# A state-space block's output: the order of its products, and kernels loaded by 8 transfers

## The chip, the cores and the metric

One core of one Trainium2 chip runs one program. The metric is the device time of one execution in microseconds (us), lower is better. TensorE (PE) multiplies, VectorE (DVE), ScalarE (ACT) and GpSimd (POOL) work element by element, SyncE (SP) issues most of the transfers between the chip's memory and SBUF, and ACT issues a few. A matrix product reads its operands from SBUF and adds into PSUM, eight banks of 128 partitions by 512 float32 each.

## The reference

Two layers; this case touches the state-space mixer of the first one. Cut to what matters:

```python
u = x.reshape(bsz, seq, 64, 16)                  # 64 groups of 16 channels, 512 positions
bu = einsum('blgh,gph->lbgp', u, B)              # complex, 64 states a group
s  = associative_scan(s_l = lambda_bar * s_{l-1} + bu_l)
y  = Re(einsum('lbgp,ghp->blgh', s, C)) + d_skip * x
h  = gelu(y)
val, gate = split(h @ w_glu, 2);  z = val * sigmoid(gate);  mix = z @ w_out
x  = layer_norm(alpha * x + mix)                 # then a SwiGLU and the second layer (attention)
```

All in float32 to a tight tolerance; the kernel splits large matrices into a high and a low part (`wh`, `wl`, `xh`, `xl`) and multiplies three times.

## The kernel before

The scan is done by chunks. The 512 positions are 64 chunks of L = 8. Within a chunk the output is a sum over at most 8 lags, a small convolution kernel; from chunk to chunk only the state is carried. The 64 groups are done in NBLK = 4 blocks of 16 groups (GB = 8 pairs: index j counts pairs, g2 picks one of the two).

For block b the steps are: `f_g`, `f_h` (DVE: tables g and h, two each), `p_t` (PE: transposes of g, ACT copies them), `p_m` (PE: input to state, into banks 2 and 3), `p_k` (PE: the lags, bank 0; ACT copies them to `ksb`; SP writes them to the DRAM scratch `kd` by two transfers, 8 groups each), `f_n` (SP reads `kd` back as the kernel tile `tn`, 128 partitions of 8 lags by 16 channels: row block n is `kd` shifted by 16 n), `f_r`, `f_s` (DVE: the scan; result `s`), `p_y` (PE: the output, banks 6 and 7; ACT copies it to `ysb` in two halves), `p_z` (PE transposes `ysb`, ACT makes the Gelu `hg` and its high part `xh`), `f_l` (DVE: the low part `xl`).

`p_y` makes, for each of 16 groups (j, g2), three products into the same 64 partitions by 128 columns of psum: step 0 is xs (the input, K = 128 rows: 8 lags by 16 channels) with `tn`; steps 1 and 2 are the real and imaginary state with h (K = 64 rows). In the profile these are the shapes 128*64 and 64*64 of L969; each float32 product is two records.

`tn` of blocks 0, 1 and 2 lies in halves of `xl` and `xh` that are not yet in use (`TNX`); that of block 3 in two ring tiles. Each of the 16 groups' kernels is read by 8 row blocks of two halves, so 16 transfers of 64 KB a block. All of them are issued by SP, but block 0's second half by ACT.

The order of the work in this stage is written out by hand as a string of letters (`SSM_ORDER`, one letter a step, the digit the block), and within the stage the scheduler keeps it on all engines:

```
"u1 u1 i1 c2 p p k1 n1 p r1 u1 u1 u1 e2 s1 g2 y1 j2 t2 T2 z1 m2 M2 h2 p i2 c3 k2 n2 u1 e3 r2 l1 p u1 u1 s2 y2 "
"g3 t3 j3 T3 z2 m3 M3 h3 i3 k3 p n3 u1 l2 r3 u1 s3 p q y3 q w0 z3 a w4 l3 q q q"
```

Between the blocks stand parts of the GLU's large products on blocks already done (u, w) and the splits of their weights (p on POOL, q on DVE: `Weights.pump`, L290 and L295). `Weights.load` (L226) issues a load as soon as a ring tile is free. Behind the stage the scheduler orders by itself: `ssm_end` (the rest of the GLU, then the output projection with the LayerNorm). `x_rev` (L1086) is the residual, which overwrites xs, so it waits until the last step 0 of block 3 has read it.

Of the kernel before, what the change touches and what calls it, by code (L numbers as in the profile page):

```python
# [22 lines left out]
L = 8  # L23
NCH = S // L
NBLK = 4
GB = 8
# [283 lines left out]
class Trunk:  # L310
# [341 lines left out]
    def ssm(self):  # L652


        tc, nc, io, ring, ws = self.tc, self.nc, self.io, self.ring, self.ws
# [27 lines left out]
        half = lambda t, i: t[:, i * NG * L:(i + 1) * NG * L].rearrange("p (a g n) -> p a g n", a=2, n=4)  # L683
# [24 lines left out]
        for hf in range(4):  # L708
# [4 lines left out]
        kd = dr.tile([NBLK, 16, 32, 240], F32, name="kd")  # L713
# [4 lines left out]
                          in_=zero.unsqueeze(1).to_broadcast([128, NBLK * 4, 112]))  # L718
# [172 lines left out]
            ring.put(ksb)  # L891

        def f_n(b):
            if b in TNX:
                half = (self.xl, self.xh)[TNX[b]][:, 4:8].rearrange("p k t -> p (k t)").bitcast(F32)
                tn = [half[:, :1024], half[:, 1024:]]
            else:
                tn = [ring.get("tn", F32) for _ in range(2)]
            for hf in range(2):
                for n in range(L):  # L900
                    (nc.scalar if b == 0 and hf else nc.sync).dma_start(
                        out=tn[hf][n * 16:(n + 1) * 16].rearrange("p (g t) -> p g t", g=8),
                        in_=kd[b, hf * 8:hf * 8 + 8, 0:16, n * 16:n * 16 + 128].rearrange("g h t -> h g t"))
            st[b]["tn"] = tn

        def f_e(b):
# [49 lines left out]
        def p_y(b):  # L956
            tn, s, h = st[b]["tn"], st[b]["s"], st[b]["h"]
            yp = self.ps[:, 6:8].rearrange("p a (j t) -> p (a j) t", j=4)
            for j in range(GB):
                for step in range(3):  # L960
                    for g2 in range(2):
                        p0, idx = g2 * 64, j * 2 + g2
                        rows = slice(p0, p0 + 64)
                        if step == 0:
                            a, m_ = xs[:, g2 * NG + b * GB + j], tn[idx // 8][:, (idx % 8) * 128:(idx % 8 + 1) * 128]
                        else:
                            a = s[rows, (step - 1) * 512 + j * 64:(step - 1) * 512 + j * 64 + 64]
                            m_ = h[step - 1][rows, j * 128:(j + 1) * 128]
                        nc.tensor.matmul(out=yp[rows, j], lhsT=a, rhs=m_, start=step == 0, stop=step == 2)  # L969
            ring.put(s, *h)  # L970
            if b not in TNX:
                ring.put(*tn)
            ysb = ring.get("ysb", F32)
            y4 = ysb.rearrange("p (i j h) -> p j i h", i=L, j=GB)
            for hf in range(2):
                js = slice(hf * 4, hf * 4 + 4)
                nc.scalar.activation(y4[:, js], yp[:, js].rearrange("p j (i h) -> p j i h", i=L), AF.Copy)
            st[b]["ysb"] = ysb
# [15 lines left out]
        def f_l(b, e=V):  # L994
            tt(self.xl[:, 2 * b:2 * b + 2], st[b]["hg2"], self.xh[:, 2 * b:2 * b + 2].bitcast(F32), SUB, e)
            ring.put(st[b]["hg"])
# [61 lines left out]
        def pump(e):  # L1058
# [3 lines left out]

        fs = dict(c=a_c, g=f_g, j=lambda b: f_g(b, 1), h=f_h, i=lambda b: f_h(b, 1), d=p_d, t=p_t,
                  T=lambda b: p_t(b, 1), m=p_m, M=lambda b: p_m(b, 1), e=f_e, k=p_k, r=f_r, y=p_y, l=f_l,
                  L=lambda b: f_l(b, G_), n=f_n, s=f_s, z=p_z,
                  B=lambda b: (powers(rest_), G_.memset(scr[0][:, 0:1], 0.0), scr_done()), b=lambda b: (levels(rest_), scr_done()))
        ET = mybir.EngineType
# [376 lines left out]
```

## Time and profile before

| | us |
|---|---|
| three runs | 1207.26, 1207.07, 1202.6 (median 1207.07) |
| the profiled execution | 1201.96 |
| its span | 1200.2 |
| `p_y` of block 0 / 1 / 2 / 3 (first L969 to the next line) | 43.80 to 51.42 / 77.78 to 85.49 / 105.68 to 113.31 / 132.09 to 139.72 |
| granted TensorE clock | 0.998 |

In a timeline line stand start, duration, engine, line, operation, output <- inputs, shape and count; in brackets the idle time of the engine before it and what ended it. In a line of stretches stand the stretch, its length, the busy time of PE, PEld (weight loads), DVE, ACT and POOL with counts, the granted clock, the DMA engines' busy share and GB/s. A line that lists a source line's instructions gives durations as min/median/max in ns and the first and last start in us.

### The profile page before, as it was taken

How to read it: one execution, taken by the hardware profiler on the slowest of the kernel's cores; microseconds unless marked ns; L12 is line 12 of the kernel's file. 1: busy time of each engine (PE TensorE's matmuls, PEld its weight loads, DVE VectorE, ACT ScalarE, POOL GpSimd, SP SyncE). 2: the span in 40 equal slices, each digit the busy share in tenths (PEclk: the TensorE clock that was granted, in tenths of full speed). 3: DMA queues.
4: the chain of work that ended last, by engine and by line, in shares of the span. 5: the costliest groups of instructions: out<-in, count | busy, mean ns of one | idle time of the engine just before them, and what ended most of it. 6: DMA issues, size and time to landing. Idle time of an engine off the chain costs nothing.

```text
span 1200.2 us, 20813 instructions
## 1 busy us (share of the span) xinstructions
PE 1156.9 (96%) x8494; PEld 1035.8 (86%) x8494; DVE 894.0 (74%) x1406; ACT 512.5 (43%) x813; POOL 378.6 (32%) x333
## 2 busy tenths in 40 slices
PE   3899999999999999999999999999999999999996
PEld 3777788899999999888887888878999999998885
DVE  8888585798788777435867787877987778884446
ACT  1355273054444445331156665653444444454300
POOL 6644402036455551001312322221254556510000
PEclk9999999999999999999999999999999999999999
DMA  5433741023323325431201121221233232264201
GB/s 199 115 81 81 233 168 47 1 89 108 122 87 121 109 90 197 137 110 66 106 13 59 54 71 53 72 88 53 89 106 123 72 123 90 88 227 141 70 18 52
DMA packets 44799, 117.91 MB, mean 98 GB/s; under 512 B 6816, under 2 KB 18080, under 8 KB 44576
## 3 DMA queue, kind: packets, MB, share of 16 engines
q1 hardware_dynamic: 43552, 116.07, 28.9%
q8 instruction: 66, 1.08, 0.4%
q10 hardware_dynamic: 1152, 0.52, 0.3%
q14 instruction: 29, 0.24, 0.1%
HBM read 112.51 MB, written 4.06 MB: 97 GB/s over the span
## 4 chain that ended last, share of the span: by engine, by line
PE 83%; DVE 10%; ACT 2%; issue 2%; POOL 2%; DMA 1%; SPq 0%; DVEq 0%; POOLq 0%; ACTq 0%
PE psum L359 16%; PE psum L361 16%; PE psum L360 16%; PE psum L378 8%; PE psum L380 8%; PE psum L379 8%; PE psum L969 2%; DVE nb L1212 1%; PE psum L1234 1%; ACT wh L290 1%; DVE wl L295 1%; PE psum L1299 1%; PE psum L1250 1%; POOL be L1213 1%; PE psum L1249 1%
## 5 line engine op out<-in xcount | busy, mean ns | idle before, releaser
L233 POOL TENSOR_TENSOR wf<-raw,wf 128x1024 fp32r<-128x1024 f32 (+1 forms) x80 | 160.0, 2015 | 128.5 <-ACT wf L246 81.6
L360 PE MATMUL psum<-xf,wf 128*128 128x256 f32 x640 | 181.4, 283 | 0.6 <-DVE wf L233 0.6
L361 PE MATMUL psum<-xf,wf 128*128 128x256 f32 x640 | 181.7, 284 | 0.0
L359 PE MATMUL psum<-xf,wf 128*128 128x256 f32 x640 | 181.5, 284 | 0.0
L295 DVE TENSOR_TENSOR wl<-raw,wh 128x1024 fp32r<-128x1024 f32 x91 | 119.6, 1325 | 59.1 <-ACT wh L290 40.3
L359 PE MATMUL psum<-xh,wh 128*128 128x512 f32 (+1 forms) x416 | 146.0, 352 | 1.8 <-ACT xh L992 1.3
L290 ACT ACTIVATE wh<-raw 128x1024 fp32r<-128x1024 f32 x108 | 112.4, 1054 | 76.1 <-PE psum L380 25.9
L361 PE MATMUL psum<-xl,wh 128*128 128x512 f32 (+1 forms) x416 | 141.4, 343 | 0.5 <-DVE xl L658 0.5
L360 PE MATMUL psum<-xh,wl 128*128 128x512 f32 (+1 forms) x416 | 141.1, 340 | 0.3 <-POOL wl L295 0.3
L380 PE MATMUL psum<-wh,hid 128*128 128x512 f32 x352 | 137.8, 392 | 0.0
L379 PE MATMUL psum<-wl,hid 128*128 128x512 f32 x352 | 137.5, 391 | 0.0
L378 PE MATMUL psum<-wh,hid 128*128 128x512 f32 x352 | 137.4, 390 | 0.0
L359 PE MATMUL psum<-xh,wf 128*128 128x256 f32 x480 | 134.9, 281 | 0.1
L361 PE MATMUL psum<-xl,wf 128*128 128x256 f32 x480 | 134.1, 279 | 0.0
L360 PE MATMUL psum<-xh,wf 128*128 128x256 f32 x480 | 134.1, 279 | 0.0
L360 PEld LDWEIGHTS psum<-xf,wf 128*128 128x128 f32 x640 | 122.3, 191 | 0.8 <-DVE wf L233 0.8
L359 PEld LDWEIGHTS psum<-xf,wf 128*128 128x128 f32 x640 | 122.6, 192 | 0.0
L361 PEld LDWEIGHTS psum<-xf,wf 128*128 128x128 f32 x640 | 122.3, 191 | 0.0
L295 POOL TENSOR_TENSOR wl<-raw,wh 128x1024 fp32r<-128x1024 f32 x17 | 41.9, 2476 | 177.0 <-DVE wl L295 96.6
L462 DVE TENSOR_TENSOR cv<-cv,psum 128x512 f32<-128x512 f32 x80 | 54.6, 683 | 48.6 <-PE psum L361 39.6
L359 PEld LDWEIGHTS psum<-xh,wf 128*128 128x128 f32 x480 | 90.5, 188 | 0.3 <-DVE hid L597 0.3
L361 PEld LDWEIGHTS psum<-xl,wf 128*128 128x128 f32 x480 | 90.3, 188 | 0.0
(227 smaller groups left out, 2679.2 us busy)
## 6 DMA issues: line engine op xcount, KB each, us to landing
raw<-w_gu SPq DMA_DIRECT2D x88, 512.0 KB, 3.4
raw<-w_down SPq DMA_DIRECT2D x44, 512.0 KB, 3.9
raw<-w_glu SPq DMA_DIRECT2D x16, 512.0 KB, 5.0
raw<-w_qk SPq DMA_DIRECT2D x16, 512.0 KB, 3.3
raw<-w_out SPq DMA_DIRECT2D x8, 512.0 KB, 3.4
raw<-w_v SPq DMA_DIRECT2D x8, 512.0 KB, 3.5
raw<-w_o SPq DMA_DIRECT2D x8, 512.0 KB, 3.2
xres<-xs SPq DMA_DIRECT2D x4, 512.0 KB, 6.9
```

Of the source, the lines that this page charges most:

```text
L233: tt = lambda o, a, b, op=SUB, e=V: e.tensor_tensor(out=o, in0=a, in1=b, op=op)
L290: nc.scalar.activation(h, w, AF.Copy)
L295: (self.l_eng or nc.vector).tensor_tensor(out=l, in0=w, in1=h.bitcast(F32), op=SUB)
L359: mm(out=out, lhsT=sh, rhs=mh, start=first, stop=False)
L360: mm(out=out, lhsT=sl, rhs=mh, start=False, stop=False)
L361: mm(out=out, lhsT=sh, rhs=ml, start=False, stop=last)
L378: mm(out=o, lhsT=sh[:, ts], rhs=hl[0][:, c], start=first, stop=False)
L379: mm(out=o, lhsT=sh[:, ts], rhs=hl[1][:, c], start=False, stop=False)
L380: mm(out=o, lhsT=sl[:, ts], rhs=hl[0][:, c], start=False, stop=last)
L462: tt = lambda o, a, b, op=ADD: V.tensor_tensor(out=o, in0=a, in1=b, op=op)
L969: nc.tensor.matmul(out=yp[rows, j], lhsT=a, rhs=m_, start=step == 0, stop=step == 2)
L1212: V.tensor_tensor_scan(nb[:, h], nb[:, h], dm[u], 0.0, MUL, ADD)
```

## The change

In `p_y` the loop over the three steps goes outside the loop over j: first all 16 products with `tn`, then 16 with the real state, then 16 with the imaginary one. The psum start flag is set for the first pair of a bank alone, the stop flag for the last. In `f_n`, blocks 0, 1 and 2 read all 16 groups in one transfer per row block: 8 transfers of 128 KB instead of 16 of 64 KB, in block 0 by turns on SP and ACT. Block 3 keeps its 16.

```diff
         def f_n(b):
+            lags = lambda gs, n: kd[b, gs, 0:16, n * 16:n * 16 + 128].rearrange("g h t -> h g t")
             if b in TNX:
                 half = (self.xl, self.xh)[TNX[b]][:, 4:8].rearrange("p k t -> p (k t)").bitcast(F32)
                 tn = [half[:, :1024], half[:, 1024:]]
+                for n in range(L):
+                    (nc.scalar if b == 0 and n % 2 else nc.sync).dma_start(
+                        out=half[n * 16:(n + 1) * 16].rearrange("p (g t) -> p g t", g=16), in_=lags(slice(0, 16), n))
             else:
                 tn = [ring.get("tn", F32) for _ in range(2)]
-            for hf in range(2):
-                for n in range(L):
-                    (nc.scalar if b == 0 and hf else nc.sync).dma_start(
-                        out=tn[hf][n * 16:(n + 1) * 16].rearrange("p (g t) -> p g t", g=8),
-                        in_=kd[b, hf * 8:hf * 8 + 8, 0:16, n * 16:n * 16 + 128].rearrange("g h t -> h g t"))
+                for hf in range(2):
+                    for n in range(L):
+                        nc.sync.dma_start(out=tn[hf][n * 16:(n + 1) * 16].rearrange("p (g t) -> p g t", g=8),
+                                          in_=lags(slice(hf * 8, hf * 8 + 8), n))
...
         def p_y(b):
-            for j in range(GB):
-                for step in range(3):
+            for step in range(3):
+                for j in range(GB):
                     for g2 in range(2):
...
-                        nc.tensor.matmul(out=yp[rows, j], lhsT=a, rhs=m_, start=step == 0, stop=step == 2)
+                        nc.tensor.matmul(out=yp[rows, j], lhsT=a, rhs=m_, start=step == 0 and j % 4 == 0,
+                                         stop=step == 2 and j % 4 == 3)
```

On PE, `p_y` of block 1 began with these rows, of which the three of L969 came eight times over (xh holds `tn`, h and s are the two operands of the state's products), ahead of the transposes L834 of the next block:

```order
L969 MATMUL psum<-xh,xres 64x128 x2
L969 MATMUL psum<-h_701,s_923 64x128 x2
L969 MATMUL psum<-h_736,s_923 64x128 x2
L834 MATMUL psum<-ident,g_929 128x128 x8
L834 MATMUL psum<-ident,g_984 128x128 x8
L984 MATMUL psum<-ident,ysb_981 128x128 x8
```

```order
L974 MATMUL psum<-xh,xres 64x128 x16
L974 MATMUL psum<-h_693,s_907 64x128 x16
L974 MATMUL psum<-h_728,s_907 64x128 x16
L834 MATMUL psum<-ident,g_913 128x128 x8
L834 MATMUL psum<-ident,g_968 128x128 x8
L990 MATMUL psum<-ident,ysb_965 128x128 x8
```

The shape changes once between the first row and the second, where it changed twice for each j; PE's order is the same everywhere else.

On SP, from block 1's writes of `kd` to block 2's reads (first as before, then as now):

```order
L888 DMA kd<-ksb_754 128x2x128 x2
L901 DMA xh<-kd 16x8x128 x16
L226 DMA raw_859<-w_glu 128x1024
L226 DMA raw_1062<-w_glu 128x1024
L888 DMA kd<-ksb_1070 128x2x128 x2
L901 DMA xl<-kd 16x8x128 x16
```

```order
L888 DMA kd<-ksb_746 128x2x128 x2
L900 DMA xh<-kd 16x16x128 x8
L226 DMA raw_843<-w_glu 128x1024
L226 DMA raw_1046<-w_glu 128x1024
L888 DMA kd<-ksb_1054 128x2x128 x2
L900 DMA xl<-kd 16x16x128 x8
```

The weight loads behind the reads now have 8 issues ahead of them where they had 16. The first read waits for both L888 rows, where it waited for the first.

On ACT, behind block 3's `p_y` (raw_1456 and raw_1686 are weight tiles just loaded, hg and xh the Gelu of block 3 and its high part):

```order
L290 ACTIVATE wh_1618<-raw_1480 128x1024
L989 ACTIVATE hg_1668<-psum 128x8x64 x2
L992 ACTIVATE xh<-hg_1668 128x1024
L290 ACTIVATE wh_1700<-raw_1559 128x1024
L290 ACTIVATE wh_1706<-raw_1565 128x1024
```

```order
L290 ACTIVATE wh_1594<-raw_1456 128x1024
L290 ACTIVATE wh_1797<-raw_1686 128x1024
L995 ACTIVATE hg_1644<-psum 128x8x64 x2
L998 ACTIVATE xh<-hg_1644 128x1024
L290 ACTIVATE wh_1676<-raw_1535 128x1024
```

One split of a weight tile has come ahead of the Gelu, and on DVE its low part ahead of block 3's `xl`. On SP the LayerNorm's scale has gone from ahead of `x_rev` to behind the two weight loads that follow it; raw_1686 is the second of these.

## Prediction

> **What bounds the kernel now.** I read the page first, then the lines of L969 (the products of `p_y`), then the timeline around each of the four places where it runs, then SP's queue.
>
> ```profile
> PE 1156.9 (96%) x8494; PEld 1035.8 (86%) x8494; DVE 894.0 (74%) x1406; ACT 512.5 (43%) x813; POOL 378.6 (32%) x333
> PE 83%; DVE 10%; ACT 2%; issue 2%; POOL 2%; DMA 1%; SPq 0%; DVEq 0%; POOLq 0%; ACTq 0%
> 150.00:200.00 50.00, 50.00 (x220) 41.05 (x219) 38.49 (x47) 30.93 (x38) 5.90 (x4) 1.00 0.38 129
> ```
>
> TensorE is the bound, and it has no idle time in the 50 us behind the state-space stage (the third line is a stretch of the trace: PE busy 50.00 of 50.00). So what PE gains before 140 us moves the end, unless another engine eats it.
>
> ```profile
> L969 PE MATMUL psum<-xl,xres x64: 272/284/324, 43.8 to 112.5; 128*64 128x128 f32 x64
> L969 PE MATMUL psum<-h,s x256: 268/270/321, 44.2 to 139.5; 64*64 64x128 f32 x128
>   issue: 12.8, 64
> 105.68 0.44 PE L969 MATMUL psum<-xl,xres 128*64 128x128 f32 x4
> 106.05 0.66 PE L969 MATMUL psum<-h,s 64*64 64x128 f32 x8
> 106.64 0.44 PE L969 MATMUL psum<-xl,xres 128*64 128x128 f32 x4
> ...
> 113.31 1.09 PE L834 MATMUL psum<-ident,g 128*128 128x128 f32 x8
> 116.55 2.09 PE L845 MATMUL psum<-xres,gt 128*64 128x64 f32 x64
> ```
>
> The first two lines give one record's duration (min/median/max ns), the third L969's idle time: 64 gaps whose releaser is "issue", 16 in each block. The others are `p_y` of block 2. One j takes 0.955 us (106.64 - 105.68 is 0.96; eight take 113.31 - 105.68 = 7.63). Its products with the kernel (L969, 128*64) are 4 records, 52 ns apart ((0.44 - 0.284)/3, 0.284 being one record); those with the state (64*64) are 8 records 55 ns apart ((0.66 - 0.27)/7): 4 x 0.052 + 8 x 0.0557 = 0.65 us. The other 0.30 us are two gaps of 0.15, one at each change between the shapes 128*64 and 64*64. It cannot be accumulation into one address: step 2 follows step 1 into the same psum with no gap, and there is a gap from j to j+1, which write different addresses.
>
> **The change part by part.** *Order.* The products and their count stay. Shape changes per block fall from 16 to 2, so 14 gaps go: 14 x 0.15 = 2.1 us by spacing, 14 x 0.2 (12.8/64) = 2.8 by the idle column. I take 2.2, near the spacing, since starts are measured and ends modelled: `p_y` then takes 5.4 us instead of 7.63. That a run of 32 equal records holds 52 ns is bounded by L845: the same shape 128*64, half the columns, 64 records in 2.09 us, 33 ns each.
>
> The copies to `ysb` lose nothing: the first half waits for step 2 of j = 3, which ends 16 records (0.85 us) before the end, and the copy takes 0.60. But step 0 of all eight j now comes first, so both halves of `tn` are needed within 0.85 us of the start, where the second half had 3.8 us.
>
> *Block 0 gains nothing.*
>
> ```profile
> 43.80 0.44 PE L969 MATMUL psum<-xl,xres 128*64 128x128 f32 x4 [1.15 <-DMA xl<-kd]
> 51.52 1.22 DVE L658 TENSOR_TENSOR g<-g,psum 128x1024 f32<-128x1024 f32 x1
> 51.42 1.09 PE L834 MATMUL psum<-ident,g 128*128 128x128 f32 x8
> 52.89 1.06 PE L834 MATMUL psum<-ident,g 128*128 128x128 f32 x8 [0.37 <-DVE g L658]
> ```
>
> The second group of transposes (T1) waits for DVE's g, done at 51.52 + 1.22 = 52.74, and DVE does not wait for `p_y`. If `p_y` ends near 49 instead of 51.4, PE idles longer before 52.89; all behind it stays. That also covers block 0's transfers up to 2 us of delay.
>
> *Transfers, block 1.* Eight of 128 KB replace sixteen of 64 KB.
>
> ```profile
> xl<-kd SPq DMA_DIRECT2D x24, 64.0 KB, 2.4
> 69.06 1.78 SPq L888 DMA_DIRECT2D kd<-ksb  x2
> L888 SPq DMA_DIRECT2D kd<-ksb x2: 377/846/1315, 69.1 to 69.5; - x2
> DMA to landing us min/median/max: 2.7/2.7/2.8
> 71.76 7.42 SPq L901 DMA_DIRECT2D xh<-kd  x16
> 37.00:37.50 0.50, 0.50 (x7) 0.50 (x6) 0.50 (x2) 0.00 (x0) 0.50 (x2) 1.00 1.01 247
> 77.78 0.44 PE L969 MATMUL psum<-xh,xres 128*64 128x128 f32 x4 [0.18 <-issue]
> 85.49 0.76 PE L834 MATMUL psum<-ident,g 128*128 128x128 f32 x5
> ```
>
> Each transfer now reads all 16 groups, so the first waits for both writes of `kd`: the second is issued at 69.5 and lands 2.7 later, 72.2, against 71.76 now. Sixteen issues take 7.42 us, 0.46 each; eight at that pace end at 72.2 + 3.7 = 75.9. But the same 1 MB must move: 247 GB/s is the most that rows of 512 B reached with all engines full (stretch 37.0 to 37.5, DMA share 1.01), so it needs at least 4.3 us, by 230 GB/s 4.6. With 0.8 until data flow and 1.1 until the landing is seen (2.4 in all for 64 KB, the first line), the last lands at 72.2 + 0.8 + 4.6 + 1.1 = 78.7. PE is there at 77.78: it waits 0.9. Bounds: 0.2 if issue alone sets it, 1.5 for a slower stream. Block 1 gains 2.2 - 0.9 = 1.3.
> [...] The trace's full engines at 247 GB/s decide, so I keep 0.9.
>
> *Block 2.* Its chain ACT `ksb` to `kd` to `tn` hangs on block 1's output, so it moves along. First issue 97.92, with the later second write some 98.3; the last lands at 98.3 + 6.5 = 104.8 on today's clock, and PE comes at 105.68 today; both move by 1.3. No wait: 2.2 more. What is late next is DVE, which moved by 1.3 only:
>
> ```profile
> 116.27 1.22 DVE L658 TENSOR_TENSOR h<-h,psum 128x1024 f32<-128x1024 f32 x1
> 118.78 0.57 PE L879 MATMUL psum<-h,g 64*32 64x112 f32 x16
> 121.67 0.59 PE L879 MATMUL psum<-h,g 64*32 64x112 f32 x16 [0.95 <-issue]
> ```
>
> `p_k` of block 3 needs the second h: ready at 117.49 - 1.3 = 116.2, used (second half of the 118.78 group) at 118.97 - 3.5 = 115.5. It waits 0.8. Later in the same `p_k` PE stands 0.95 us for "issue"; if that runs on during the wait, nothing is lost, else 0.8. I take half: 0.4.
>
> *Block 3 gains nothing.* It keeps 16 transfers, first half first.
>
> ```profile
> 132.09 0.44 PE L969 MATMUL psum<-tn,xres 128*64 128x128 f32 x4 [1.38 <-DMA tn<-kd]
> 135.90 0.44 PE L969 MATMUL psum<-tn,xres 128*64 128x128 f32 x4
> L901 SPq DMA_DIRECT2D tn<-kd x16: 303/428/431, 125.1 to 132.1; - x16
> DMA to landing us min/median/max: 2.5/3.2/3.8
> 139.72 0.50 PE L359 MATMUL psum<-xh,wh 128*128 128x512 f32 x1
> ```
>
> The last issue at 132.1 lands at 135.3 (134.6 to 135.9): hidden now, as j = 4 starts at 135.90. After, on the same clock, step 0 of j = 4 wants it at 132.94 and waits to 135.3; then 0.85 + 0.15 + 3.4 us remain, ending at 139.7, where it ends today. The gaps saved become a wait for `tn`; the bound is 0.6 either way.
>
> *Behind the stage.* ACT's split of a later weight now stands ahead of z3's Gelu.
>
> ```profile
> 139.24 0.33 SPq L1086 DMA_DIRECT2D xres<-x_rev  x1
> 143.81 0.33 SPq L226 DMA_DIRECT2D raw<-w_glu  x1
> DMA to landing us min/median/max: 3.1/4.2/10.1
> 148.08 1.04 PE L984 MATMUL psum<-ident,ysb 128*128 128x128 f32 x8
> 148.87 0.48 PE L359 MATMUL psum<-xh,wh 128*128 128x512 f32 x1
> 154.47 0.39 PE L359 MATMUL psum<-xh,wh 128*128 128x512 f32 x1
> 149.16 2.12 ACT L989 ACTIVATE hg<-psum 128x512 f32<-128x512 f32 x2 [7.78 <-PE psum L984]
> 152.40 1.23 DVE L658 TENSOR_TENSOR xl<-hg,xh 128x1024 fp32r<-128x1024 f32 x1 [8.62 <-ACT xh L992]
> ```
>
> The third line is the landing of the `raw` loads between 120 and 175 us. On today's clock that load is issued at 143.81 and lands at 148.0, the split takes 1.05, and the Gelu could start at 149.1, as it does. xl ends at 153.6. PE has 24 products from 148.87 that don't need block 3; the 25th, at 154.47, needs its xh, the 27th, 0.46 us later, its xl: 1.3 us of delay are covered. Cost 0. x_rev, its wait on `p_y`'s step 0 now ending early, goes ahead of it by more than before, which helps. Other moves on SP, DVE and ACT there are hidden by the 50.00 of 50.00.
>
> Sum: 0 - 1.3 - 2.2 + 0.4 + 0 + 0 = -3.1 us. The profiled execution took 1201.96 us (span 1200.2): 1198.9. The three runs shown are 1207.26, 1207.07 and 1202.6; from their median it would be 1204.0. Both levels occur twice in the four executions, so I put 1202 between them.
>
> **The rivals.** *Issue takes longer for 128 KB (slower).* The second 128 KB write of `kd` took SP 1.315 us, the first 0.377. Its place: `tn` of blocks 1 and 2. At t per issue the last lands at 72.2 + 7t + 2.7 in block 1, a wait of 7t - 2.9, and 7t - 4.6 in block 2. It eats the 4.4 us gained from t = 0.85 on; at 1.3 it costs 6.2 + 4.5 - 4.4 = +6.3, 1208.3. Against it: kd's first write and 64 KB loads at 0.43. Chance 0.16 that waits eat most of the gain (time near 1202), a quarter of it really slower.
>
> *Z3's weight load lands late.* At the 10.1 us seen, 153.9 instead of 148.0, PE would stand 5.9 - 1.3 = 4.6 us: +1.5, 1203.5. Against it: x_rev leaves sooner. Chance 0.08.
>
> *The clock drops in block 0.* PE would idle about 2.4 us before 52.89 around a 1.09 us burst.
>
> ```profile
> 55.00:59.00 4.00, 2.57 (x66) 2.00 (x62) 2.13 (x3) 3.04 (x3) 0.78 (x2) 1.00 0.00 0
> ```
>
> Here PE is busy 2.57 of 4.00 us and the clock granted is 1.00. At half clock the work from 52.89 to 56.84 would take up to 4 us longer: +0.9, 1202.9. Chance 0.04.
> [...]
>
> *More is on the path.* If gaps cost 0.2 (2.8 a block), no `tn` wait grows and block 3 gains as well: 3 x 2.8 = 8.4 less 1 for DVE, 1194.6. Against it: the 247 GB/s and the 135.3. Chance 0.11.
>
> **How the numbers follow.** The forecast (-1 to -5.5 us) has 0.61. What a measurement can tell here is about 0.5%, 6 us: nearly all of the forecast lies inside it. Faster by more: most of the last rival and a little of the forecast, 0.13. Slower by more: a quarter of the first, some of the next two and an unseen cost of the moved weight splits, 0.08. Same: 0.79. Range: 1195 (last rival) to 1209 (the upper level with +2); the forecast's own is 1196.5 to 1206.
>
> **What would show it.** L969's gaps for "issue" fall from 64 to about 8, and `p_y` takes 5.4 us in blocks 0 to 2. PE waits for `xh<-kd` some 0.9 us in block 1 and for the second `tn` some 2.4 us inside block 3's step 0; T1 of block 0 still starts at 52.9. The start of z3's transposes moves from 148.1 to 145.0. The forecast is wrong if products of one shape run slower than 55 ns, if the eight issues take over 6 us, or if PE waits behind 150 us.

## The result and the profile after

The changed kernel took 1215.35 us (median of 4 runs, 1213.41 to 1216.26) against 1205.86 for the kernel before (4 runs, 1202.6 to 1207.26). The ratio is 1.0091 [1.0075, 1.0107]: slower by 0.9%, about 9.5 us, where I had forecast 3 us less and a range that ended at 1209. The profiled execution took 1215.46 us with a span of 1213.6, 13.4 us more than the 1200.2 before.

The page of the changed kernel first: PE's busy time, then the clock granted to PE in 40 slices, where the third and the last had been a 9. Below it are lines of the answer on L974, the products of `p_y` (L969 before): the time of one record, and what ended the idle time in front of it.

```profile
PE 1154.8 (95%) x8494; PEld 1042.2 (86%) x8494; DVE 895.2 (74%) x1406; ACT 512.1 (42%) x813; POOL 379.5 (31%) x333
PEclk9989999999999999999999999999999999999998
L974 PE MATMUL psum<-xh,xres x32: 421/421/474, 84.5 to 87.8; 128*64 128x128 f32 x32
  issue: 21.2, 7
  DMA tn<-kd: 4.0, 2
  DMA xl<-kd: 3.9, 1
```

PE's work is the same (1154.8 against 1156.9 us). The answer on a line counts PE and its weight loads (PEld) together. Of the 64 small gaps for "issue" before, 63 (12.6 of 12.8 us) were idle time of the weight loads; PE itself stood 0.2 us for "issue" and 2.6 for kernels. Now PE stands 5.8 us in one gap for "issue", 7.9 for kernels and 2.0 in block 0 (below); the other 15.4 of the 21.2 us belong to the weight loads. A record of block 1 took 421 ns instead of 283: the work itself ran slower.

The four places in PE's timeline, block 0 to block 3 (start, length, operation, count; in brackets the idle time ahead and what ended it):

```profile
43.68 1.97 PE L974 MATMUL psum<-xl,xres 128*64 128x128 f32 x32 [2.01 <-DMA raw<-w_glu]
52.71 1.94 PE L834 MATMUL psum<-ident,g 128*128 128x128 f32 x8 [2.41 <-DVE g L658]
84.54 3.68 PE L974 MATMUL psum<-xh,xres 128*64 128x128 f32 x32 [5.78 <-issue]
88.15 4.45 PE L974 MATMUL psum<-h,s 64*64 64x128 f32 x64
92.53 1.09 PE L834 MATMUL psum<-ident,g 128*128 128x128 f32 x8
116.63 3.36 PE L974 MATMUL psum<-xl,xres 128*64 128x128 f32 x32 [3.94 <-DMA xl<-kd]
123.78 1.09 PE L834 MATMUL psum<-ident,g 128*128 128x128 f32 x8
143.32 1.09 PE L974 MATMUL psum<-tn,xres 128*64 128x128 f32 x16 [1.78 <-DMA tn<-kd]
146.61 1.09 PE L974 MATMUL psum<-tn,xres 128*64 128x128 f32 x16 [2.19 <-DMA tn<-kd]
147.63 5.38 PE L974 MATMUL psum<-h,s 64*64 64x128 f32 x64
152.94 0.50 PE L359 MATMUL psum<-xh,wh 128*128 128x512 f32 x1
```

PE stands 5.78 us ahead of block 1 and 3.94 ahead of block 2; the 5.78 is marked "issue", but the answer on the tile `xh` lists it as a wait for the transfers into `xh`. Block by block, on the two clocks: `p_y` of block 1 ends at 92.53 instead of 85.49 (+7.0), of block 2 at 123.78 instead of 113.31 (+10.5), and the first product behind block 3 starts at 152.94 instead of 139.72 (+13.2). z3's transposes start at 161.30 instead of 148.08, +13.2 again. So the whole loss arises in the state-space stage; the span is 13.4 us longer, so only 0.2 us is added behind 153 us.

The transfers and the clock in block 1: SP's eight issues (the landing row is that of all 128 KB transfers), then the changed kernel in steps of 2 us, and last a stretch of before. The last three columns are the clock granted to PE, the DMA engines' busy share, and GB/s.

```profile
73.38 3.76 SPq L900 DMA_DIRECT2D xh<-kd  x8
DMA to landing us min/median/max: 3.2/5.6/7.9
76.00:78.00 2.00, 2.00 (x11) 1.63 (x10) 1.98 (x2) 1.18 (x2) 2.00 (x3) 1.00 1.26 113
80.00:82.00 2.00, 0.00 (x0) 0.00 (x0) 2.00 (x3) 0.32 (x1) 1.95 (x3) 1.00 1.26 121
84.00:86.00 2.00, 1.46 (x14) 1.49 (x16) 2.00 (x3) 0.00 (x0) 0.00 (x0) 0.50 0.94 377
86.00:88.00 2.00, 2.00 (x22) 1.82 (x18) 1.79 (x2) 0.00 (x0) 0.00 (x0) 0.50 0.00 0
```
```profile
76.00:78.00 2.00, 1.81 (x11) 1.18 (x10) 2.00 (x3) 0.97 (x2) 2.00 (x3) 1.00 0.61 137
```

The eight issues took 3.76 us, half of the sixteen before. But the megabyte then moved at 113 to 121 GB/s with the engines' share at 1.26, where the old transfers moved 137 at 0.61: more busy and slower. The last one is in at about 84.5 us, 11.2 us after the first issue. By then PE has stood for 5.78 us, and its clock is halved (0.50 from 84 to 88 us).

### The profile page after: what moved, and what is told of

It is laid out like the page before. It is cut to its first block, busy times and chain, and to the rows that moved or that the text cites. A ratio compares the mean times of both kernels' runs of the same rounds, so it can differ in the third digit from the quotient of the medians.

```text
span 1213.6 us, 20779 instructions
## 1 busy us (share of the span) xinstructions
PE 1154.8 (95%) x8494; PEld 1042.2 (86%) x8494; DVE 895.2 (74%) x1406; ACT 512.1 (42%) x813; POOL 379.5 (31%) x333
## 4 chain that ended last, share of the span: by engine, by line
PE 81%; DVE 10%; DMA 2%; ACT 2%; POOL 2%; issue 2%; SPq 1%; DVEq 0%; POOLq 0%; ACTq 0%
PE psum L359 15%; PE psum L361 15%; PE psum L360 15%; PE psum L378 8%; PE psum L380 8%; PE psum L379 8%; PE psum L974 2%; DVE nb L1218 1%; PE psum L1240 1%; DVE wl L295 1%; PE psum L1256 1%; PE psum L1305 1%; POOL be L1219 1%; PE psum L879 1%; ACT wh L290 1%
## 5 line engine op out<-in xcount | busy, mean ns | idle before, releaser
L359 PEld LDWEIGHTS psum<-xh,wf 128*128 128x128 f32 x480 | 90.4, 188 | 0.0
L360 PEld LDWEIGHTS psum<-xh,wf 128*128 128x128 f32 x480 | 90.2, 188 | 0.0
```

Of the source, the lines that this page charges most:

```text
L359: mm(out=out, lhsT=sh, rhs=mh, start=first, stop=False)
L360: mm(out=out, lhsT=sl, rhs=mh, start=False, stop=False)
```

## The experiments

The runs had three questions: which of the two parts costs the time, what the dropped clock costs by itself, and why a transfer of 128 KB is slow. Theory T throughout: the slow transfers and the clock they bring down cost everything, and the new order is worth its gaps. The main rival: the order itself costs.

**The order alone.** `f_n` is taken back to 16 transfers of 64 KB; `p_y` stays as changed.

```diff
-                    (nc.scalar if b == 0 and n % 2 else nc.sync).dma_start(   # 8 of 128 KB
+                    (nc.scalar if b == 0 and hf else nc.sync).dma_start(      # 16 of 64 KB
```

> The new order of the products with the old 16 transfers of 64 KB. Theory T (the loss is the 128 KB loads, which land at 102 to 121 GB/s, plus the clock that drops after PE's wait for them): xh lands near 81.6 us as before, so PE waits about 3 us for the second half inside step 0 of block 1 and 1.3 in block 2; these eat most of the 2.2 us of gaps per block, and a dropped clock may add up to 2 us: 1206 to 1210, at least 5 us below the changed kernel. Rival R (the order itself costs, the loads only show it): within 3 us of the changed kernel's 1215.

It took 1209.11 us beside 1204.58 for before: 1.0032 [1.0017, 1.0047]. In PE's timeline of block 1:

```profile
78.91 1.09 PE L970 MATMUL psum<-xh,xres 128*64 128x128 f32 x16
83.45 1.97 PE L970 MATMUL psum<-xh,xres 128*64 128x128 f32 x16 [3.45 <-issue]
85.35 4.45 PE L970 MATMUL psum<-h,s 64*64 64x128 f32 x64
```

Step 0 now wants the second half of the kernel 0.9 us after the first and waits 3.45 us for it; then its products run at half the speed (1.97 us for 16 records, where 16 took 1.09). T's figure holds. The order as written is a small loss even with the old transfers, because it puts the operand that lands last at the front.

**The loads alone.** The order is taken back, the 8 transfers stay.

```diff
-            for step in range(3):
-                for j in range(GB):
+            for j in range(GB):
+                for step in range(3):
...
+                        ... start=step == 0, stop=step == 2)
```

> The new 8 transfers of 128 KB with the old order of the products. T: the whole of tn again lands near 84.5 us, PE waits about 6.8 us ahead of block 1 and 3 to 4 ahead of block 2, no gaps are saved, the clock drops after both waits: 1217 to 1223, slower than the changed kernel. R: within 3 us of before's 1206.

1216.99 us, 1.0106 [1.0083, 1.0128], at the low end of T's range; the rival is out. PE waits 5.04 us in block 1 and 3.35 in block 2, where T had 6.8 and 3 to 4. The first product of block 1 has this row:

```profile
82.35 0.70 PE L973 MATMUL psum<-xh,xres 128*64 128x128 f32 x4 [5.04 <-issue]
```

So the loads alone cost about what the whole change does. With them in place the change's order makes no difference that can be told: 1.0091 and 1.0106 with overlapping intervals.

**The state first.** Old transfers, shape changes as few as in the change, but the products with the kernel come last.

```diff
-            for step in range(3):
+            for step in (1, 2, 0):
...
-                        ... start=step == 0 and j % 4 == 0, stop=step == 2 and j % 4 == 3)
+                        ... start=step == 1 and j % 4 == 0, stop=step == 0 and j % 4 == 3)
```

> Old transfers, and in every block the 32 products with the state first, those with the kernel tn last (two shape changes, tn wanted 3.5 us later). T: p_y takes 5.4 us instead of 7.63, no wait for tn in any block; block 0 gains nothing, blocks 1 and 2 gain 2.2 each less 0.5 for DVE's h, block 3 gains 2.2 and 1.2 of its 1.38 us wait: about -7, 1199. R: as slow as the order alone, 1206 or more.

1197.76 us, 0.9939 [0.992, 0.9958]: 6.8 us faster than before, where 7 were expected.

```profile
78.70 3.71 PE L970 MATMUL psum<-h,s 64*64 64x128 f32 x64
82.34 1.97 PE L970 MATMUL psum<-xh,xres 128*64 128x128 f32 x32
84.24 1.09 PE L834 MATMUL psum<-ident,g 128*128 128x128 f32 x8
128.43 3.71 PE L970 MATMUL psum<-h,s 64*64 64x128 f32 x64 [0.72 <-ACT part L1023]
132.07 1.97 PE L970 MATMUL psum<-tn,xres 128*64 128x128 f32 x32
```

`p_y` takes 84.24 - 78.70 = 5.54 us and waits for no kernel, in block 3 either, where before had stood 1.38 us. The state was there first: in this run DVE ends s at 73.7 us in block 1, 5 us ahead, and in block 3 it ends the half of s that the first 32 records read at 128.3, just ahead of 128.43. Fewer shape changes are worth what the prediction said; they were paired with the wrong operand.

**The state first, with the 8 transfers.** The same edit on the changed kernel.

```diff
-            for step in range(3):
+            for step in (1, 2, 0):
```

> State products first, as e3_state_first, but with the changed kernel's 8 transfers of 128 KB. T: tn of block 1 still lands near 84 us; the state products fill PE up to 82.4, so PE waits about 2 us instead of 5.78 and its clock holds; in block 2 the wait is under 1 us; block 3 is as in e3_state_first. So the loads cost 2 to 4 us over e3_state_first: 1199 to 1202 beside before at 1204.7, where the same loads cost 6 us between e1_order and the changed kernel. Rival (the loads harm something else as well, for example the raw weight loads behind them): 1205 or more.

1201.18 us beside 1204.13: 0.9974 [0.9965, 0.9984]. PE waits 3.44 us instead of 5.78 in block 1 (below) and 0.1 in block 2. T's time holds, its wait of 2 us was too small.

```profile
85.88 1.97 PE L974 MATMUL psum<-xh,xres 128*64 128x128 f32 x32 [3.44 <-issue]
```

**The clock by itself.** The changed kernel with idle products (`p_d`, ident by ident, result unused) in PE's waits, and some between the halves of block 3's step 0 (not in the lines below). Two runs; in the first they were twice too long.

```diff
-    "... y0 g1 t1 j1 T1 ... s1 g2 y1 ... s2 y2 ... p q y3 ..."
+    "... y0 g1 t1 j1 d9 d9 T1 ... s1 g2 d9 d9 d9 d9 y1 ... s2 d9 d9 d6 y2 ... p q d8 y3 ..."      # first run
+    "... y0 g1 t1 j1 d8 T1 ... s1 g2 d9 d9 y1 ... s2 d9 d3 y2 ... p q d4 y3 ..."                  # second run
```

> The changed kernel with idle products of ident with ident (0.115 us apart, result unused) in PE's waits: 18 ahead of T1 of block 0, 36 ahead of block 1's p_y, 24 ahead of block 2's, 8 ahead of block 3's and 14 between the halves of its step 0. T with the clock as its own term: the waits stay (84.5 us, 3 to 4 us in block 2), the granted clock stays at 1.00, and 2.6 (block 1), 1.8 (block 2), 1.8 (block 3) and up to 1.2 us (block 0) come back: 1207.5 to 1210. Rival: the clock has nothing to do with PE's idle time, or costs nothing on the path: 1214 to 1217.

1217.38 us: a miss, since the filler itself held PE back (first two lines; `p_y` of block 1 starts at 90.26 instead of 84.54).

> As e4_warm, with idle products that fit the waits (e4_warm's trace has one such product at 0.23 us, two records, not 0.115: they overran the waits and p_y of block 1 began at 90.26 instead of 84.54): 8 ahead of T1 of block 0, 18 ahead of block 1's p_y, 12 ahead of block 2's, 4 ahead of block 3's and 7 between the halves of its step 0. T: p_y begins where it does in the changed kernel, the granted clock stays 1.00 from 76 to 155 us, and 2.6 + 1.8 + 1.8 us come back, up to 1.2 more in block 0: 1207.5 to 1210. Rival (the clock costs nothing on the path): 1214 to 1217.

1206.25 us beside 1204.74, 1.0014 [0.9999, 1.0029]: more came back than T's 1207.5 to 1210. The other lines are of this run:

```profile
82.03 8.30 PE L852 MATMUL psum<-ident 128*128 128x128 f32 x72 [0.69 <-ACT part L1029]
90.26 1.97 PE L976 MATMUL psum<-xh,xres 128*64 128x128 f32 x32
```
```profile
81.51 4.29 PE L852 MATMUL psum<-ident 128*128 128x128 f32 x36 [0.69 <-ACT part L1029]
85.73 1.97 PE L976 MATMUL psum<-xh,xres 128*64 128x128 f32 x32
87.62 3.71 PE L976 MATMUL psum<-h,s 64*64 64x128 f32 x64
91.27 1.09 PE L834 MATMUL psum<-ident,g 128*128 128x128 f32 x8
84.00:86.00 2.00, 2.00 (x22) 1.88 (x22) 2.00 (x3) 0.00 (x0) 0.01 (x1) 1.00 0.95 303
```

`p_y` of block 1 starts 1.2 us later than in the changed kernel and ends 1.3 us earlier, since its 96 records take 5.54 us at clock 1.00 instead of 7.99. Filling the waits with nothing useful took the time from 1.0091 to 1.0014 of before: some 9 us, 5 to 13 by the two intervals. The price of the clock by the rows of the changed kernel is 7.99 - 5.54 = 2.45 in block 1, 7.15 - 5.54 = 1.6 in block 2, 5.38 - 3.71 = 1.7 in block 3 and up to 1.2 in block 0, about 7: more than half of the loss. In the execution shown, which took 1210.55 us, block 0 gave nothing back: the first product behind it starts at 59.76, against 59.32 in the changed kernel.

**The state first, with filler in block 0.** There `e3_state_first` still shows slow transposes behind two waits of 1.83 and 2.47 us.

```diff
-    "... y0 g1 t1 j1 T1 ..."
+    "... y0 g1 d5 t1 j1 d8 T1 ..."
```

> e3_state_first with 5 idle products ahead of the first and 8 ahead of the second group of transposes of block 0, where its PE stands 1.83 and 2.47 us and the transposes then take 1.94 instead of 1.06 us. If the clock costs there what it seems to: z0 and what follows 1.2 us earlier, 1196.5. Rival: DVE's g and ACT's Gelu set that stretch anyway, or the idle products wait for ACT's copy of psum bank 7 and push the transposes back: 1197.8 or more.

1194.76 us, 0.9919 [0.9904, 0.9934], 1.7 us below the 1196.5 expected. The first product behind the block starts at 58.20 instead of 59.32, as expected, and the clock between 53 and 55 us is 1.00 instead of 0.50. This is the fastest version of the study; its interval overlaps that of `e3_state_first`.

```profile
53.00:55.00 2.00, 2.00 (x22) 1.83 (x24) 2.00 (x2) 1.16 (x3) 2.00 (x3) 1.00 0.00 0
```

**Why 128 KB is slow: the old size on two queues.** `f_n` again with 64 KB, by SP and ACT in turns.

```diff
+                        (nc.scalar if n % 2 else nc.sync).dma_start(out=tn[hf][n * 16:(n + 1) * 16]...
```

> The changed kernel with the old 16 transfers of 64 KB, issued by SP and ACT in turns in blocks 1 and 2 too: the old size at twice the rate of issue. H1 (the engines fall behind as soon as transfers are issued faster than they are served, whatever their size): DMA share near 1.26 and 110 to 130 GB/s while tn streams in block 1, as with 128 KB. H2 (the form of 128 KB, 16 rows of 512 B per partition, is slow in itself): share near 0.6 to 0.9 and 200 GB/s or more. ACT also waits for kd here, so its time is not compared.

```profile
74.00:76.00 2.00, 0.00 (x0) 0.00 (x0) 1.97 (x3) 0.00 (x0) 0.00 (x0) 1.00 1.14 200
76.00:78.00 2.00, 0.00 (x0) 0.00 (x0) 2.00 (x2) 0.00 (x0) 0.00 (x0) 0.82 1.19 149
```

132 to 200 GB/s at a share of 1.1 to 1.2: neither H1's 110 to 130 nor H2's full speed. This run settles neither.

**Loads by themselves.** Three kernels with nothing but loads of 1 MB; DVE sums each, and its wait for the next (the bracket) is the time of one load.

```diff
+ lambda: old([SP]), lambda: new([SP]), lambda: old([SP, ACT]), lambda: new([SP, ACT]),   # old: 16x8 rows, new: 16x16 rows
+ lambda: new([ACT], 1), apart, wide, long_rows, lambda: old([SP]), lambda: new([SP])
...
+ nc.vector.tensor_reduce(out=red[:, i:i + 1], in_=tn, axis=mybir.AxisListType.X, op=ADD)   # behind each
```

> Nothing but loads of 1 MB, each followed by a DVE sum that the next one waits for; kd is filled with ones and no part of the model is computed. In this order: (1) 16 of 64 KB on SP as before; (2) 8 of 128 KB on SP as changed; (3) as 1 on SP and ACT in turns; (4) as 2 on SP and ACT; (5) as 2 on ACT with a copy of 128x1024 between two issues; (6) as 2, from 8 places of kd that do not overlap; (7) 16 of 64 KB with one row of 512 B in each of 128 partitions; (8) 8 of 128 KB to 16 partitions, each 8 KB in one piece; (9) and (10) as 1 and 2 again. H1: 1 about 137 GB/s, 2, 3, 4 all near 115 at share 1.26, 5 near 115 to 130 at share 0.6 with landings of 2.5 us. H2: 3 faster than 1, 5 as slow to land as 2. H3 (reads of the same DRAM rows by neighbouring transfers collide): 6 at 200 or more where 2 has 115. If 16 partitions at a time are what is slow, 7 is fast and 6 and 8 are not.

Loads 2 (as changed), 3, 6 and 9 (as before):

```profile
32.64 2.29 DVE L212 TENSOR_REDUCE red<-tn 128x1 f32<-128x2048 f32 x1 [11.20 <-DMA tn<-kd]
43.12 2.29 DVE L212 TENSOR_REDUCE red<-tn 128x1 f32<-128x2048 f32 x1 [8.20 <-DMA tn<-kd]
82.43 2.29 DVE L212 TENSOR_REDUCE red<-tn 128x1 f32<-128x2048 f32 x1 [11.11 <-DMA tn<-kd]
118.40 2.29 DVE L212 TENSOR_REDUCE red<-tn 128x1 f32<-128x2048 f32 x1 [9.59 <-DMA tn<-kd]
```

The slowness is there with nothing else running on the core: 11.20 against 9.59 us. H1 falls (the old form on two queues, issued faster, is the fastest of the ten at 8.20; the new form on two queues, load 4, takes 9.25), and so does H3 (reads that don't overlap: 11.11).

```diff
+ nc.sync.dma_start(out=tn[p0:p0 + parts, r0 * 128:(r0 + rows) * 128].rearrange("p (r t) -> p r t", r=rows), in_=v[k, :, :, 0:128])
```

> As m1_loads, loads of 1 MB in rows of 512 B alone, all issued by SP, to find what of the form makes 128 KB slow (m1_loads: 11.2 us from first issue to the sum, whether the rows overlap or not; 9.3 with one row in each of 128 partitions, 8.2 with the old form on two queues). In this order, partitions x rows of one transfer: (1) 16x16 as changed, (2) 16x16 from rows that do not overlap, (3) 32x8, (4) 64x4, (5) 128x2, (6) 128x4 (256 KB), (7) 128x16 (1 MB at once), (8) 8x16 (64 KB), (9) 16x8 (64 KB). P (an engine works through one partition's rows in sequence, and few partitions mean few engines at full rate): 3 to 7 faster than 1, the more the wider, 5 under 8 us; 8 slower than 9. B (bytes of one transfer alone decide): 3, 4, 5 as slow as 1 (11 us), 6 and 7 no faster, 8 like 9.

Loads 2, 3, 5, 7 and 8, that is 16x16, 32x8, 128x2, 128x16 and 8x16:

```profile
34.88 2.29 DVE L202 TENSOR_REDUCE red<-tn 128x1 f32<-128x2048 f32 x1 [11.14 <-DMA tn<-kd]
45.44 2.29 DVE L202 TENSOR_REDUCE red<-tn 128x1 f32<-128x2048 f32 x1 [8.27 <-DMA tn<-kd]
65.74 2.29 DVE L202 TENSOR_REDUCE red<-tn 128x1 f32<-128x2048 f32 x1 [7.69 <-DMA tn<-kd]
82.55 2.29 DVE L202 TENSOR_REDUCE red<-tn 128x1 f32<-128x2048 f32 x1 [5.98 <-DMA tn<-kd]
102.19 2.29 DVE L202 TENSOR_REDUCE red<-tn 128x1 f32<-128x2048 f32 x1 [17.35 <-DMA tn<-kd]
```

At the same 128 KB, 16 partitions take 11.14 us, 32 take 8.27 and 128 take 7.69; B falls. The last load, 9, isn't compared: its sixteen issues took 0.60 us each and set its time.

```diff
+ nc.sync.dma_start(out=tn[p0:p0 + (parts - 1) * by + 1:by].rearrange("p (r t) -> p r t", r=16), in_=v[parts][k, :, :, 0:128])
```

> Loads of 1 MB alone as in m2_forms, all issued by SP, 16 rows of 512 B per partition throughout; only which partitions one transfer writes is changed. In this order: (1) 16 neighbouring partitions, (2) 16 partitions 8 apart, (3) 16, 4 apart, (4) 16, 2 apart, (5) as 1 again, all 8 x 128 KB; (6) 8 neighbouring, (7) 8, 16 apart, (8) 8, 4 apart, 16 x 64 KB. [...] If an engine's rows of one partition in sequence set it: 2, 3, 4 as slow as 1 (11 us), 7 and 8 as slow as 6 (17 us).

Loads 2 and 4 (16 partitions, 8 and 2 apart; load 3, 4 apart, waits 8.25), 5 (16 neighbours) and 6 (8 neighbours):

```profile
31.74 2.29 DVE L196 TENSOR_REDUCE red<-tn 128x1 f32<-128x2048 f32 x1 [8.19 <-DMA tn<-kd]
52.79 2.29 DVE L196 TENSOR_REDUCE red<-tn 128x1 f32<-128x2048 f32 x1 [8.23 <-DMA tn<-kd]
66.70 2.29 DVE L196 TENSOR_REDUCE red<-tn 128x1 f32<-128x2048 f32 x1 [11.62 <-DMA tn<-kd]
86.06 2.29 DVE L196 TENSOR_REDUCE red<-tn 128x1 f32<-128x2048 f32 x1 [17.07 <-DMA tn<-kd]
```

The same bytes in the same rows to the same number of partitions take 8.2 us when these are spread, and 11.62 when they are neighbours. An engine's rows of one partition in sequence don't set it, then: by that, loads 2 to 4 would have taken 11 too. For these loads alone that decides it: which partitions a transfer writes sets its rate. While they stream, 16 neighbours moved 111 to 117 GB/s (load 1, 13 to 19 us), 16 partitions 8 apart 178 to 229 (load 2, 26 to 30 us) and 8 neighbours 69 to 72 (load 6, 74 to 80 us). No run here shows what makes neighbours slow. The kernel itself was not run with spread partitions; its 11.2 us in block 1 are what the load alone takes (11.20 in `m1_loads`). Loads 7 and 8 (8 partitions, 16 and 4 apart) took 12.97 and 13.46 us, of which their sixteen issues of 0.57 and 0.65 us make up 9 and 10. They do show that 8 partitions at a time need not take 17.

One thing stays open. The old form writes the same 16 neighbours and moves 137 GB/s, where that of 128 KB moves 113 to 121. Several of its short transfers, to different partitions, are under way at once (issued 0.46 us apart, 2.5 to land at the median), but that alone doesn't tell the two forms apart: those of 128 KB are issued 0.45 us apart and take 5.6 to land, so they overlap too. No run here isolates the reason.

## Why the prediction was wrong, point by point

*Shape changes: right.* A block with 2 instead of 16 takes 5.54 us at full clock (block 0 of the changed kernel, all of `e3_state_first`), where 5.4 was said, and a product keeps its spacing (32 records with the kernel in 1.97 us and 64 with the state in 3.71, 54 and 55 ns apart). The 14 changes saved took 2.09 us with them, 0.15 each, as the spacing had it. The 0.2 each "by the idle column" was no second measure of it, since 63 of those 64 gaps are idle time of the weight loads.

*Block 0: right in its waits, not in its price.* T1 starts at 52.71 (52.89 before, "stays"). But PE's 2.41 us of idle time ahead of it brought the clock to 0.50 between 53 and 55 us: the transposes took 1.94 instead of 1.06, and the first product behind the block starts 1.2 us later. I had this as a rival with a chance of 0.04 and a price of 0.9. I argued from 55 to 59 us of the kernel before, where PE was busy 2.57 of 4.00 us and kept its clock. Here it was busy 1.59 of 4.00 (1.31 ahead of the wait, the rest behind it). The first stretch of the changed kernel holds the wait, the second the slow products:

```profile
49.00:53.00 4.00, 1.59 (x16) 1.22 (x13) 3.97 (x5) 1.72 (x4) 4.00 (x4) 0.89 0.00 0
53.00:55.00 2.00, 2.00 (x11) 2.00 (x10) 1.97 (x3) 0.91 (x2) 2.00 (x3) 0.50 0.03 8
```

*Block 1: the step that failed.* "The last lands at 78.7, PE waits 0.9", bounds 0.2 to 1.5. It landed near 84.5 and PE waited 5.78. The issue term was right (3.76 us for eight); the stream was not. From the first issue to the last landing the sum had 0.8 + 4.6 + 1.1 = 6.5 us, and it took 11.2 (73.38 to 84.54). The first issue came 1.2 us later than the sum's 72.2, too, behind block 0's slow transposes: in `e2_loads`, where these took 1.06 us, PE's first product behind the block comes at 57.86 instead of 59.32. I took 230 GB/s from the best half microsecond, 247 GB/s, of block 0's load on two queues. One microsecond on, the same load of the kernel before looks like this:

```profile
38.00:39.00 1.00, 1.00 (x11) 1.00 (x10) 0.96 (x2) 0.00 (x0) 0.91 (x3) 1.00 1.26 134
```

That is a share above 1 at a low rate, just what block 1 then showed, and I read past it. A rate for a megabyte has to come from a stretch about as long as the megabyte takes. The bound "1.5 for a slower stream" had no row behind it.

*Block 2: the same step.* "No wait" came from moving 1 MB in 6.5 us; it takes about 11, and PE waited 3.94.

*The clock in the waits: left out.* The sum had a price for PE's standing still, and none for what PE does after it. The waits of blocks 1 to 3 were followed by half-speed products that cost 1.6 to 2.45 us each; block 0's price stands above.

*Block 3: right in its wait.* The second half of `tn` was waited for 2.19 us (2.4 said), which eats the gaps saved; the 1.7 us lost there are again the clock.

*The 0.4 us for h in block 3's `p_k`: not put to the test.* Block 2's `p_y` was late, so h was ready at 124.5 us, and the products that use it start behind 129 us. In `e8_first_loads`, nearer to the forecast's times, PE waits 0.38 us for it.

*Behind the stage: right.* z3's transposes are 13.2 us late, as is everything ahead of them, and no more.

*The rival of slow 128 KB issues* named the right place and the right wait (blocks 1 and 2, for `tn`) and a price of 6.3 us, by a mechanism that didn't occur: an issue took 0.446 us, as I had it. What grew was the time from issue to landing, 2.5 to 5.6 us at the median, which I had carried over from 64 KB.

## What to carry to other kernels

Before making transfers fewer and larger, ask which partitions one of them writes: sixteen neighbours took 11 us for a megabyte where spread or wider ones took 6 to 8.3. In an accumulation, put first the products whose operands are ready and last those whose operand lands last; here that order, with the old loads, turned +0.9% into -0.6%. And price a wait of the matrix engine twice: for its length, and for the slow products behind it (5.78 and 2.45 us in block 1).

## What the runs showed of the hardware beyond that

A wait can cost more than itself. After 5.78 and 3.94 us of idle time PE ran at half clock for about 5 and 3.4 us. Shorter waits can go either way. Behind 3.45 us in `e1_order` the clock was 0.50 from 84 to 86 us, while 3.44 in `e8_first_loads` left it at 1.00 throughout 82 to 88 us. Behind waits of 1.3 and 0.5 us near 60 us, products of 128x512 that otherwise come 0.23 us apart came 0.43 apart in `e1_order` (from 59.7 to 62.7) and in `e5_warm` (from 62.2 to 65.1); behind the same waits in the kernels before and after they came 0.23 apart, at a clock of 1.00. In block 0 of the changed kernel it fell within the wait of 2.41 us: it was 1.00 from 51.5 to 52.0 and 0.66 from 52.0 to 52.5, so it fell about 1.9 us after PE's last product, which ended at 50.31. The length of the wait alone doesn't tell which way it goes, and no run here isolates what does.
